# Rebalancing two on-chip rings and the transfer order in a matmul-scale-add kernel: a 16-tile x ring with casts six tiles ahead, a 32-tile add_value ring, eight-tile transfers

## The chip, the cores and the metric

One core of one Trainium2 chip. The time is the device time of one execution in microseconds (us); where several runs were made, their median is given with the lowest and highest. The profile's span (first to last instruction) is 1.7 to 2.1 us shorter than the time. Kernels that are compared ran on the same chip in the same rounds where that is said, and otherwise the spread is told.

## The reference

```python
# x: 16 x 512 x 1024, weight: 1024 x 768, add_value: 16 x 512 x 768, all fp32
def reference(x, weight, scale, add_value):
    return (scale * np.matmul(x, weight) + add_value).astype(np.float32)
```

Flattened, x has 8,192 rows: 64 tiles of 128. All of x (33.6 MB), weight (3.1), add_value (25.2) and the result (25.2) cross the DMA engines once, 87.03 MB in all.

## The kernel before

All transfers go through one issuing queue (SyncE), in the order of a list. Each entry is an operand, its first tile and the number of tiles: x loads, w weight chunks, a add_value loads, o outputs, l and r the two column parts of the last tile's output.

```python
STREAM = [
    ("x", 0, 1), ("x", 1, 1), ("x", 2, 1), ("w", 0, 1), ("w", 1, 1), ("w", 2, 1),
    ("w", 3, 1), ("w", 4, 1), ("w", 5, 1), ("x", 3, 1), ("w", 6, 1), ("w", 7, 1),
    ("a", 0, 3), ("a", 3, 1), ("x", 4, 4), ("x", 8, 4), ("a", 4, 4), ("x", 12, 4),
    ("a", 8, 8), ("x", 16, 8), ("a", 16, 8), ("x", 24, 8), ("o", 0, 8), ("x", 32, 8),
    ("a", 24, 4), ("a", 28, 4), ("o", 8, 8), ("x", 40, 4), ("a", 32, 8), ("o", 16, 8),
    # ... the same pattern on to tile 63
]
X_SLOTS = 24      # ring of x tiles, fp32
A_SLOTS = 24      # ring of add_value tiles; the result is written in place
```

A step is one tile. TensorE transposes the next tile in the middle of a step (through PSUM, ScalarE copies it out); for pairs of tiles (14 and 15, 19 and 20, ...) VectorE does the transposing instead. GpSimd casts x to bf16 ahead of either.

```python
def step():
    t = done["step"]
    for j in range(KJ):                                   # 8 contraction steps
        if j == KJ // 2:
            if t + 1 not in in_pair:
                transpose(t + 1)                          # TensorE, needs the cast of t + 1
            cast_to(min(t + 2, done["x"] - 1))            # GpSimd, frees a slot of the x ring
            if t + 7 in PAIRS:
                cast_pair(t + 7)
        product(t, j, BOTH)                               # 512 + 256 columns
    finish(t, BOTH[0], 0, N)                              # VectorE: scale, add, into the a ring
    # VectorE turns a quarter of a coming pair
```

An x load waits until the tiles in its slots are cast; an add_value load waits until the outputs in its slots have left.

## Time and profile before

| | before |
|---|---|
| time (3 runs) | 211.96 us (211.57 to 212.16) |
| TensorE busy | 196.4 us, 93% of the span |
| DMA engines busy | 98.1% of 16 engines |
| first steady transposes on TensorE | 26.33 us |
| last output: issued, time to landing | 206.53, 3.0 us |

The lines behind this table are in the prediction below. Two resources are near full, so the question for any change is which of them sets the end.

### The profile page before, as it was taken

What the parts mean: (1) busy time and instruction counts of PE and PEld (TensorE: products, weight loads), DVE (VectorE), ACT (ScalarE), POOL (GpSimd) and SP (SyncE); (2) the same over time, 40 slices, a digit from 0 to 9 for tenths busy, and PEclk for the clock granted to TensorE, in tenths of its full rate; (3) what the DMA queues carried; (4) which work ended last, traced back from release to release, by engine and by line L of the source; (5) the groups of instructions that cost most, each with busy time, mean ns of one, the idle gap of its engine ahead of it and who ended that gap; (6) DMA issues with size and microseconds to landing.
All of it is one profiled execution on the core that took longest, in us unless ns stands there. A gap on an engine that the chain in (4) does not pass through costs nothing.

```text
span 210.4 us, 3034 instructions
## 1 busy us (share of the span) xinstructions
PE 196.4 (93%) x1218; PEld 119.5 (57%) x1218; DVE 131.0 (62%) x223; ACT 49.3 (23%) x52; POOL 63.8 (30%) x69
## 2 busy tenths in 40 slices
PE   7887099999999999999999999999999999999991
PEld 2444056665656566666566565656665665666650
DVE  1447212329969869649999499786984993332232
ACT  3503013323302303112113023031121130233320
POOL 1310253441090080540350901705407340233000
PEclk9999759999999999999999999999999999999997
DMA  6999999999999999999999999999999999999995
GB/s 220 391 417 439 417 422 434 445 455 427 405 455 431 406 444 442 395 413 444 416 417 410 439 413 442 417 419 428 411 455 408 448 408 438 434 406 428 430 405 202
DMA packets 6781, 87.22 MB, mean 414 GB/s; under 512 B 752, under 2 KB 880, under 8 KB 2928
## 3 DMA queue, kind: packets, MB, share of 16 engines
q1 hardware_dynamic: 6768, 87.03, 98.1%
q8 instruction: 9, 0.15, 0.3%
q14 instruction: 4, 0.03, 0.0%
HBM read 61.87 MB, written 25.17 MB: 414 GB/s over the span
## 4 chain that ended last, share of the span: by engine, by line
PE 85%; DMA 10%; SPq 1%; POOL 0%; ACT 0%; issue 0%; DVE 0%; POOLq 0%; ACTq 0%
PE mm L168 76%; PE tp L146 9%; DMA xs<-in_x_dram 7%; DMA ao<-in_weight_dram 4%; SPq L100 1%; SPq L248 1%; POOL xb L136 0%; ACT xt L152 0%; DVE ao L176 0%; POOLq L136 0%; ACTq L152 0%
## 5 line engine op out<-in xcount | busy, mean ns | idle before, releaser
L168 PE MATMUL mm<-w_bf,xt 128*128 128x512 bf16 (+1 forms) x736 | 130.0, 330 | 1.9 <-DVE w_bf L104 1.4
L168 PEld LDWEIGHTS <-xt 128*128 128x128 bf16 x736 | 69.2, 99 | 52.2 <-ACT xt L152 10.8
L176 DVE SCALAR_TENSOR_TENSOR ao<-mm,ao 128x768 f32<-128x768 f32 (+2 forms) x62 | 58.4, 945 | 60.8 <-PE mm L168 43.8
L152 ACT COPY xt<-tp 128x1024 bf16<-128x1024 bf16 (+1 forms) x49 | 46.6, 961 | 150.7 <-PE tp L146 150.7
L120 DVE STREAM_TRANSPOSE vt<-vx 32x256 f32<-32x256 f32 x144 | 62.7, 435 | 2.7 <-POOL vx L109 0.5
L136 POOL CAST xb<-xs 128x1024 bf16<-128x1024 f32 x43 | 43.6, 1040 | 45.8 <-PE tp L146 26.4
L168 PE MATMUL mm<-w_bf,vt 128*128 128x512 bf16 (+1 forms) x288 | 49.7, 326 | 0.0
L109 POOL CAST vx<-xs 128x1024 bf16<-128x1024 f32 x18 | 18.2, 1040 | 78.7 <-DVE vt L120 45.0
L168 PEld LDWEIGHTS <-vt 128*128 128x128 bf16 x288 | 28.1, 98 | 17.6
L146 PE MATMUL tp<-identity,xb 128*128 128x128 f32 x184 | 28.9, 282 | 6.5 <-POOL xb L136 5.8
L146 PEld LDWEIGHTS tp<-identity,xb 128*128 128x128 f32 x184 | 22.2, 145 | 13.1 <-POOL xb L136 6.2
L104 DVE CAST w_bf<-ao 128x768 bf16<-128x768 f32 x8 | 4.5, 565 | 4.7 <-DMA ao<-in_weight_dram 4.7
L94 PE MATMUL warm<-zeros 128*128 128x512 bf16 x10 | 4.4, 629 | 1.2 <-DVE zeros L82 1.2
L132 DVE CAST xb<-xs 128x512 bf16<-128x512 f32 x3 | 1.3, 427 | 5.4 <-DMA xs<-in_x_dram 5.4
L134 POOL CAST xb<-xs 128x512 bf16<-128x512 f32 x2 | 1.7, 866 | 5.2 <-DMA xs<-in_x_dram 5.2
L94 PEld LDWEIGHTS <-zeros 128*128 128x128 bf16 x10 | 1.3, 140 | 3.4 <-issue 2.2
L235 DVE TENSOR_TENSOR ao<-ao 128x768 f32<-128x768 f32 x3 | 2.7, 952 | 0.0
L204 DVE TENSOR_SCALAR ao<-mm 128x768 f32<-128x768 f32 x2 | 1.8, 953 | 1.1 <-PE mm L168 1.1
L134 ACT ACT_TABLE_LOAD x1 | 1.3, 1283 | 0.7 <-PEq L279 0.7
L134 ACT CAST xb<-xs 128x512 bf16<-128x512 f32 x1 | 0.6, 618 | 2.5 <-DMA xs<-in_x_dram 2.5
L201 ACT ACTIVATE ao<-mm 128x768 f32<-128x768 f32 x1 | 0.8, 817 | 0.0
L82 DVE MEMSET zeros<- 128x256 uint32 x1 | 0.3, 272 | 0.9 <-PEq L279 0.9
(6 smaller groups left out, 0.9 us busy)
## 6 DMA issues: line engine op xcount, KB each, us to landing
out_dram<-ao SPq DMA_DIRECT2D x7, 3072.0 KB, 23.5
xs<-in_x_dram SPq DMA_DIRECT2D x9, 2048.0 KB, 23.8
ao<-in_add_value_dram SPq DMA_DIRECT2D x6, 3072.0 KB, 12.4
xs<-in_x_dram SPq DMA_DIRECT2D x3, 4096.0 KB, 42.3
ao<-in_add_value_dram SPq DMA_DIRECT2D x3, 1536.0 KB, 16.7
ao<-in_weight_dram SPq DMA_DIRECT2D x8, 384.0 KB, 7.8
xs<-in_x_dram SPq DMA_DIRECT2D x4, 512.0 KB, 5.1
out_dram<-ao SPq DMA_DIRECT2D x1, 1536.0 KB, 10.6
```

Source lines behind the costliest of these rows:

```text
L94: nc.tensor.matmul(warm[:, 0:CUT], zeros[:, 0:P], zeros, start=True, stop=True)
L100: nc.sync.dma_start(ao[:, s, :], w_v[:, j // 2, j % 2, :])
L104: nc.vector.tensor_copy(w_bf[:, j + i, :], ao[:, s + i, :])
L109: nc.gpsimd.tensor_copy(vx[:, i, :], xs[:, (t0 + i) % X_SLOTS, :])
L120: nc.vector.transpose(vt[b:b + 32, :, 32 * a:32 * a + 32], pairs[32 * a:32 * a + 32, :, b:b + 32])
L134: other(xb[:, K // 2:K], src[:, K // 2:K])
L136: nc.gpsimd.tensor_copy(xb, src)
L146: nc.tensor.transpose(tp[:, c, :], pairs[:, c * P:(c + 1) * P], identity)
L152: nc.scalar.copy(dst[:, c:c + q, :, :], src[:, c:c + q, :, :])
L168: nc.tensor.matmul(mm_tiles[t, cols[0]][:, n0:n1], lhs(t, j), w_bf[:, j, n0:n1], start=(j == 0), stop=(j == KJ - 1))
L176: nc.vector.scalar_tensor_tensor(a, mm_tiles[t, part][:, n0:n1], float(scale), a, op0=mybir.AluOpType.mult, op1=mybir.AluOpType.add)
L235: nc.vector.tensor_add(ao[:, t, :], ao[:, EARLY_AT + t, :], ao[:, t, :])
```

## The change

The intent: the same SBUF with the two rings rebalanced. Casting six tiles ahead into seven bf16 buffers frees x slots early, so 16 fp32 slots do; the freed space makes the add_value ring 32 tiles. The transfers are made uniform, eight tiles each, and the head of the list is merged.

```diff
 STREAM = [
-    ("x", 0, 1), ("x", 1, 1), ("x", 2, 1), ("w", 0, 1), ... , ("w", 5, 1), ("x", 3, 1), ("w", 6, 1), ("w", 7, 1),
-    ("a", 0, 3), ("a", 3, 1), ("x", 4, 4), ("x", 8, 4), ("a", 4, 4), ("x", 12, 4),
-    ...
+    ("x", 0, 3), ("w", 0, 2), ("w", 2, 2), ("w", 4, 2), ("x", 3, 1), ("w", 6, 2),
+    ("a", 0, 3), ("x", 4, 4), ("a", 3, 1), ("x", 8, 4), ("a", 4, 4), ("x", 12, 4),
+    ("a", 8, 8), ("x", 16, 8), ("a", 16, 8), ("x", 24, 8), ("a", 24, 8), ("o", 0, 8),
+    ("x", 32, 8), ("a", 32, 8), ("x", 40, 8), ("o", 8, 8), ("x", 48, 8), ("a", 40, 8),
+    ("o", 16, 8), ("o", 24, 8), ("a", 48, 8), ("x", 56, 8), ("a", 56, 8), ("o", 32, 8),
+    ("o", 40, 8), ("o", 48, 8), ("o", 56, 4), ("o", 60, 1), ("o", 61, 1), ("o", 62, 1),
+    ("l", 63, 1), ("r", 63, 1),
 ]
-X_SLOTS = 24
-A_SLOTS = 24
+X_SLOTS = 16
+A_SLOTS = 32
+AHEAD = 6
@@
-    xb_pool = ... bufs=3
+    xb_pool = ... bufs=7
@@
-                    cast_to(min(t + 2, done["x"] - 1))
+                    cast_to(min(t + AHEAD, done["x"] - 1))
```

## The prediction

> **What bounds the kernel now.** I read the page first: its engine shares, its 40-slice picture and its DMA queue table.
>
> ```profile
> PE 196.4 (93%) x1218; PEld 119.5 (57%) x1218; DVE 131.0 (62%) x223; ACT 49.3 (23%) x52; POOL 63.8 (30%) x69
> ...
> DMA  6999999999999999999999999999999999999995
> ...
> q1 hardware_dynamic: 6768, 87.03, 98.1%
> ```
>
> Two resources are full at once: TensorE for 93% of the span, the 16 DMA engines for 98.1% (206.4 of 210.4 us). The DMA row has no slice below 9 except the first and the last, so no gap in the transfers is there to be closed. TensorE has its gap at the front. The chain of waits, in order of time, shows it:
>
> ```profile
> 3.73 7.51 DMA ao<-in_weight_dram
> 11.26 13.83 DMA xs<-in_x_dram
> 25.24 1.05 POOL xb L136
> 26.33 1.11 PE tp L146 x4
> 27.45 4.31 PE mm L168 x16
> 31.76 0.44 PE tp L146 x4
> 32.19 2.63 PE mm L168 x16
> ```
>
> The first four-tile x transfer lands at 25.09 us (11.26 + 13.83). GpSimd casts tile 4, TensorE transposes it at 26.33, and from there TensorE runs almost without a break to 206.05; over 40 to 200 us the stretch table gives 159.83 us busy of 160. The first step is slow (4.31 instead of 2.63 us), at a clock of 0.50 between 25 and 30 us.
>
> Which of the two sets the end is read from the tail. The last output (128 KB) is issued at 206.53, after the last matmul and VectorE's last add. The DMA view of 206.4 us to the end says:
>
> ```profile
> DMA packets 363, 0.59 MB, mean 129 GB/s; under 512 B 47, under 2 KB 175, under 8 KB 363
> ...
> out_dram<-ao SPq DMA_DIRECT2D x1, 128.0 KB, 3.0
> ```
>
> Only 0.13 MB is issued in this stretch, but 0.59 MB still has to start: 0.46 MB stands ahead of the last transfer. At the 425 GB/s of the stretch 5 to 205 us that is 1.1 of its 3.0 us to landing. So with an empty queue the compute side alone would have landed near 206.53 + 3.0 - 1.1 = 208.4; the DMA queue makes it 209.5. **The DMA engines are the bound, by about 1.1 us over TensorE.** Both have to move for a gain above that.
>
> The longest waits in the issuing queue look alarming and are not:
>
> ```profile
> SPq L254 <- DMA out_dram<-ao: 118.6, 5, 32.3
> SPq L262 <- DVE ao L176: 34.2, 7, 9.0
> ```
>
> The first is an add_value load waiting until the output in its slots has left. Meanwhile earlier transfers are still being moved: x transfers take 24 to 42 us from issue to landing, of which a 2 MB one needs 5 us at 425 GB/s. Waiting in the issuing queue costs nothing while that backlog lasts.
>
> **What the Trainium skill says.** "DMA: Bandwidth & Descriptors", Specifications, gives a fabric ceiling of 435 GB/s. The trace agrees: 425 GB/s is held for 200 us, so at most 2% is to be won from the transfers by any means. "Perfetto Trace Analysis", What "DMA-bound" means, says that for a bound on the DMA engines large descriptors matter. The trace has the size of it, in the packet records: a 3,072-byte packet takes 121 ns in the median, 4,096 bytes 159, 12,288 bytes 460, 24,576 bytes 912, 32,768 bytes 1,214. That is a line: 8.4 ns a packet and 27.2 bytes per ns. "TensorE: Matmul & The Clock Gate", Part 1, says the clock drops after an idle window of about 3.4 us; here TensorE idles 5.8 us before 26.33 and the clock is 0.50 after it. "SBUF — State Buffer", Who interferes with whom, lets GpSimd and VectorE block each other on a shared port in some operations. I see nothing of that: GpSimd's cast is 1,040 to 1,042 ns in all 61 instances although VectorE is 62% busy. Moving casts earlier should not lengthen them.
>
> **The change part by part.**
>
> *Transfers.* Bytes stay the same. Before there are 47 transfers; after it 38: x goes from 16 to 11, weights from 8 to 4, add_value from 11 to 10, outputs from 12 to 13 (tiles 60 and 61 part). A transfer has 128 rows, so 8 packets on each of 16 engines, plus a semaphore packet of 9 ns. Nine fewer take 9 x (8 x 8.4 + 9) = 0.69 us off every engine's work. This lies directly on what sets the end: 209.5 becomes about 208.8.
>
> *Head.* The first x transfer is now 1.5 MB, so its casts start near 7 us (2.5 us later than tile 0's at 4.50). The weights come in pairs at nearly the same times as before, and the last still lands near 16 us, since the bytes ahead are the same. So the head's matmuls end near 19 us either way. The four add_value tiles used to be ahead of the first four-tile x; now the fourth goes behind it. That brings it forward by 0.375 MB, 0.97 us by the landings of like transfers, and and the head has six fewer transfers ahead of it, 0.46 us. TensorE's stream starts 1.4 us earlier, near 24.9. A shorter idle could also keep some clock: up to 1.7 us, the excess of 4.31 over 2.63. So compute alone would land at 207.0 or earlier (208.4 - 1.4), which is now 1.8 us inside the DMA bound. Most of it is not cashed in.
>
> *Casts six ahead.* The number of casts (43 + 18, 1,040 ns each) is the same; GpSimd is at 30%. Of the idle time of TensorE only 5.8 us is put down to a cast, and that is the one at 26.33, set by the landing. Worth 0 by itself; it makes a ring of 16 possible: a slot is free six tiles ahead of use, so 16 + 6 = 22 tiles of reach stand against 24 + 2 = 26.
>
> *Add_value ring of 32.* It breaks the wait of 118.6 us in part: tiles 24 to 31 no longer wait for the first output. Their load moves from 81 us to near 43. Worth 0 while the queue is never empty, but VectorE's waits for add_value (13.6 us in 4 cases, longest 4.2) shrink or move.
>
> **Does the queue ever run dry?** This decides between a small gain and a loss. I walked the new order by hand with first in, first out at the rates above and TensorE steps of 2.63 or 3.07 us. The tight places are where a load waits with little behind it. x 48 to 55 needs the casts of tiles 32 to 39, of which pair 39 and 40 waits for VectorE to turn pair 34, so it is issued near 114 us; the queue has work until about 120. Add_value 40 to 47 waits for output 8 to 15, landing near 122; x 48 fills the queue until about 130. x 56 and add_value 48 come near 146, work lasts until about 152. Each has 5 to 8 us in hand. The one data wait that can touch TensorE is add_value 40 to 47, landing near 139 when step 40 is done near 136; three PSUM buffers cover that by 2 to 3 us, but VectorE turns pair 44 behind it, which leaves under 1 us before step 44 needs it.
>
> **Rivals.**
> 1. *TensorE takes over or its head gain shows in full.* If the tail backlog were a small thing, the end would follow TensorE: 1.4 us, with the clock up to 3 us earlier, 209 to 210.5. The 0.46 MB ahead of the last output speak against it. The bytes cannot go faster.
> 2. *The smaller x ring starves the queue.* x loads in pieces of eight wait for eight casts. With 5 to 8 us in hand, a step or two of delay is absorbed; only a chain of delays at 114 or 146 us would open a gap, costing 2 to 5 us, 213 to 217.
> 3. *The late add_value 40 blocks VectorE and then TensorE.* The kernel before has the like: VectorE waited 4.24 us at 187 and TensorE did not stop. Costs 1 us of TensorE at most, hidden by the 1.8 us.
> 4. *Larger transfers in the tail or head cost latency.* The outputs of the tail are split finer, not coarser; the head has slack. Near zero.
>
> **Range and chances.** The span falls by 0.7 us, from 210.4 to 209.7; the measured time from 211.96 to **211.2 us** after rounding. The low end, 209.9, is rival 1 in part, with the slowest DMA engine faring better: in the tail the semaphore of the last of the 16 comes 1.3 us after the median one, which may differ by program. The high end, 212.3, is no gain and a scatter like the 211.57 to 212.16 of before. Faster by over 2% would need 207.7, beyond what 87 MB allow at the ceiling together with the head: 0.02. Slower by over 2% needs 216.2, a dry queue for 4 us: 0.05. Within 2%: 0.93.
>
> **What will show it.** Right: 9 x (128 + 16) = 1,296 fewer packets, DMA share near 98% with no slice below 9 inside; the first step's transposes near 24.9 us; TensorE ending near 204.6; the last output landing 3.5 us or more after its issue, behind a larger backlog. Wrong: a slice of the DMA row under 9 near 115 to 122 or 146 to 152 (rival 2), a TensorE gap near 139 to 146 (rival 3), or a last output that lands 2 us after issue, which would say that the transfers were not the bound. A longer median packet time for the 32,768-byte rows would break the packet sum.

## The result, and the profile after

The changed kernel takes 210.96 us (210.62 to 211.10, 4 runs), the kernel before in the same rounds 211.99 us (211.57 to 212.16). The ratio is 0.9952, 95% interval 0.9933 to 0.9971. Ratios here are the mean time of one kernel's runs over that of the other's of the same rounds, so not quite the ratio of the medians.

From the page of the changed kernel: TensorE's busy time, the DMA row of the 40 slices, and the queue's packets and share.

```profile
PE 196.4 (94%) x1218; PEld 119.5 (57%) x1218; DVE 131.1 (63%) x223; ACT 49.3 (24%) x52; POOL 63.2 (30%) x69
...
DMA  6999999999999999999999999999999999999993
...
q1 hardware_dynamic: 5472, 87.03, 97.7%
```

The work of TensorE is the same, and again no slice of the DMA row inside is below 9. The packets fell from 6,768 to 5,472, the 1,296 that nine fewer transfers make. The share fell by little, but of a shorter span: 97.7% of 209.2 us is 204.4 us, against 206.4 before.

The chain of waits of the changed kernel at the start of the steady stream:

```profile
20.67 2.61 DVE ao L235 x3
23.29 1.02 POOL xb L136
24.36 0.66 PE tp L146 x4
25.01 4.28 PE mm L168 x16
29.29 0.44 PE tp L146 x4
29.73 2.63 PE mm L168 x16
```

TensorE's stream starts at 24.36 us, 1.97 earlier. The line ahead of the cast names VectorE, but what the cast needs is the x transfer, which the trace has landing at 23.21. The first step is still slow (4.28 us), the next ones take 2.63 us as before. TensorE ends its matmuls at 203.6 instead of 206.0 us; VectorE's last add comes right behind, in the kernel before and then in the changed kernel:

```profile
206.07 0.42 DVE ao L176
...
203.61 0.42 DVE ao L176
```

The DMA view of the changed kernel from 203.9 us, just before its last output is issued at 204.06, to the end:

```profile
DMA packets 449, 0.81 MB, mean 132 GB/s; under 512 B 58, under 2 KB 186, under 8 KB 449
...
out_dram<-ao SPq DMA_DIRECT2D x1, 128.0 KB, 4.1
```

Now 0.81 MB still has to start when the last 0.13 MB is issued (0.59 MB before), and the last output takes 4.1 us (3.0 before). TensorE finished 2.4 us earlier; the last output landed only 1.34 us earlier (208.20 against 209.54). The rest of TensorE's gain went into a longer queue.

### The profile page after: what moved, and what is told of

Read it like the earlier page. It is cut to its first block, busy times and chain, and to the rows that moved or that the text cites. A ratio compares the mean times of both kernels' runs of the same rounds, so it can differ in the third digit from the quotient of the medians.

```text
span 209.2 us, 2988 instructions
## 1 busy us (share of the span) xinstructions
PE 196.4 (94%) x1218; PEld 119.5 (57%) x1218; DVE 131.1 (63%) x223; ACT 49.3 (24%) x52; POOL 63.2 (30%) x69
## 3 DMA queue, kind: packets, MB, share of 16 engines
q1 hardware_dynamic: 5472, 87.03, 97.7%
## 4 chain that ended last, share of the span: by engine, by line
PE 90%; DMA 3%; DVE 2%; ACT 1%; POOL 0%; issue 0%; ACTq 0%; POOLq 0%
PE mm L168 80%; PE tp L146 10%; DMA xs<-in_x_dram 3%; DVE ao L235 1%; ACT xt L152 1%; DVE ao L204 1%; POOL xb L136 0%; DVE xb L132 0%; DVE ao L176 0%; ACTq L152 0%; POOLq L136 0%
## 5 line engine op out<-in xcount | busy, mean ns | idle before, releaser
L152 ACT COPY xt<-tp 128x1024 bf16<-128x1024 bf16 (+1 forms) x49 | 46.6, 961 | 146.0 <-PE tp L146 146.0
L136 POOL CAST xb<-xs 128x1024 bf16<-128x1024 f32 x43 | 43.2, 1040 | 56.2 <-DMA xs<-in_x_dram 46.5
L109 POOL CAST vx<-xs 128x1024 bf16<-128x1024 f32 x18 | 18.3, 1040 | 53.8 <-DVE vt L120 44.7
L146 PE MATMUL tp<-identity,xb 128*128 128x128 f32 x184 | 28.3, 277 | 5.4 <-POOL xb L136 3.0
L146 PEld LDWEIGHTS tp<-identity,xb 128*128 128x128 f32 x184 | 21.7, 143 | 12.1 <-POOL xb L136 3.4
L132 DVE CAST xb<-xs 128x512 bf16<-128x512 f32 x3 | 1.9, 696 | 5.6 <-DMA xs<-in_x_dram 5.6
```

Of the source, the lines that this page charges most:

```text
L109: nc.gpsimd.tensor_copy(vx[:, i, :], xs[:, (t0 + i) % X_SLOTS, :])
L136: nc.gpsimd.tensor_copy(xb, src)
L146: nc.tensor.transpose(tp[:, c, :], pairs[:, c * P:(c + 1) * P], identity)
L152: nc.scalar.copy(dst[:, c:c + q, :, :], src[:, c:c + q, :, :])
```

## The experiments

Theory A: the DMA engines are the bound, and a transfer costs its bytes plus a small fixed cost for each packet. Theory B: TensorE's stream is the bound, and its earlier start is the gain. Two questions came up on the way: what the cast-ahead is worth (theory C), and what scatters the kernel before (D and E).

### Which resource sets the end: three cuts

Each run takes work from one side of the changed kernel, or from both. Their outputs are wrong, which doesn't matter for the times.

```diff
     def product(t, j, cols):
+        end = KJ - 2 if 20 <= t < 40 else KJ - 1      # e1, e3
+        if j > end:
+            return
...
         elif op == "a":
+            if s == 40:                               # e2, e3
+                continue
```

> The changed kernel with the last of the eight contraction steps left out for tiles 20 to 39 (results of these tiles wrong on purpose): 20 x 0.33 = 6.6 us less TensorE work, the same transfers. Theory A (the DMA engines are the bound): the time stays at 210.9 us within 0.4. Theory B (TensorE's stream is the bound): it falls by 2 us or more, up to 6.6.

> The changed kernel without the load of add_value tiles 40 to 47 (wrong on purpose): 3.1 MB, 7.3 us of all DMA engines, less; TensorE's work the same. Theory A: the time falls until TensorE takes over, by the share of the last output's 4.1 us to landing that is queue, about 2.0 to 2.4 us, to 208.6 to 209.0, and the last output lands about 2 us after its issue. Theory B: no change.

> Both cuts of the first two runs together (wrong on purpose). Theory A: now both bounds move, the time falls by 5 to 7 us, more than the sum of the two single cuts. Theory B: falls by as much as with TensorE's cut alone.

| run | TensorE's matmuls | transfers | time (4 runs) | against 210.93 |
|---|---|---|---|---|
| changed kernel, once more (6 runs, other rounds) | | | 210.93 (210.63 to 211.05) | |
| e1 | -6.6 us | | 210.89 (210.69 to 210.98) | 0.0 |
| e2 | | -3.1 MB | 208.46 (208.19 to 208.69) | -2.5 |
| e3 | -6.6 us | -3.1 MB | 205.91 (205.72 to 206.19) | -5.0 |

The DMA view of e2 from 203.4 us, just before its last output is issued at 203.55, to the end:

```profile
DMA packets 289, 0.39 MB, mean 60 GB/s; under 512 B 33, under 2 KB 161, under 8 KB 289
...
out_dram<-ao SPq DMA_DIRECT2D x1, 128.0 KB, 1.8
```

With TensorE's work cut the time does not move. With the transfers cut it falls, to a little under the 208.6 to 209.0 us expected, until the tail queue is gone: the last output lands 1.8 us after its issue, with its own and the previous tile part's bytes alone left to start. Both cuts together give twice the sum of the single ones. Theory A holds and B falls: the DMA engines are the bound, with 2.5 us to TensorE's bound behind it.

The cut of 6.6 us did not make TensorE's stream 6.6 us shorter. In e3 (as in e1) the steps that transpose the next tile still follow each other every 3.07 us, because TensorE now waits for ScalarE's copy of the transposed tile:

```profile
92.83 0.60 PE L146 MATMUL tp<-identity,xb 128*128 128x128 f32 x4
...
94.59 1.48 PE L171 MATMUL mm<-w_bf,xt 128*128 128x512 bf16 x8 [0.18 <-ACT xt L152]
95.90 0.60 PE L146 MATMUL tp<-identity,xb 128*128 128x128 f32 x4
```

Only the eight steps of this stretch in which TensorE transposes nothing get shorter: 8 x 0.33 = 2.6 us by estimate. That is what e3 shows (its last output is issued at 201.10 us, 2.45 us before that of e2), and why it gains 5.0 us and not up to 7. In e1 TensorE is 2.3 us ahead at step 38 and loses it again near 140 us, behind add_value 40 to 47. So B was tested with 2.3 us, of which nothing was left in the time.

### What a packet costs: the same bytes in more transfers

```diff
-    ("a", 8, 8), ("x", 16, 8), ...
+    ("a", 8, 4), ("a", 12, 4), ("x", 16, 4), ("x", 20, 4), ...      # all 20 eight-tile transfers
```

> The changed kernel with each of its 20 eight-tile transfers issued as two of four tiles: bytes and order the same, 20 more transfers. Packet theory (8.4 ns for each packet plus 9 ns for each transfer on every engine): 20 x 0.076 = 1.5 us longer, 212.4 us. Rival (only bytes count, and the gain of the change came from the earlier start of TensorE): no change within 0.3 us.

It took 212.12 us (211.99 to 212.31), 1.23 us over e1 of the same rounds and 1.2 over the changed kernel. The packet theory's 1.5 us is right in kind and a quarter too large. The packet records show the engines' mean busy time up by 1.6 us (206.26 against 204.62 in the changed kernel's second profile); why not all of that reaches the time is not shown. The rival, that only bytes count, falls.

### The parts of the change alone

e5 is the changed kernel again; e6 the kernel before with the new head of the list (its first two lines in the diff above); e7 the changed kernel with the old head; e8 the changed kernel with five further merges (and a line of the head's test that the merged x load needs).

```diff
 e8:
+    ("x", 0, 4), ("w", 0, 2), ("w", 2, 2), ("w", 4, 2), ("w", 6, 2),
+    ("x", 4, 4), ("a", 0, 4), ("x", 8, 4), ("a", 4, 4), ("x", 12, 4),
...
-    ("o", 56, 4), ("o", 60, 1), ("o", 61, 1), ("o", 62, 1), ("l", 63, 1), ("r", 63, 1),
+    ("o", 56, 6), ("o", 62, 1), ("o", 63, 1),
```

> The changed kernel once more, beside the parts of the change on the same chip: 1.0 us under the kernel before, 0.6 to 1.3.

> The kernel before with the changed head alone (first x tiles in one transfer, weights in pairs, the fourth add_value tile behind the first four-tile x): six transfers fewer, TensorE starts about 2 us earlier. Packet theory: 6 x 0.076 = 0.46 us under the kernel before. TensorE theory: 1.4 to 2 us under it.

> The changed kernel with the old head: three transfers fewer than before in the middle and the tail, TensorE starts as late as before. Packet theory: 3 x 0.076 = 0.23 us under the kernel before, and together with the head alone the whole of the change. TensorE theory: as the kernel before.

> The changed kernel with five more transfers merged (x 0 to 3 in one, add_value 0 to 3 in one, outputs 56 to 61 in one, tile 63 in one), the first four-tile x ahead of add_value. Packet theory: 5 x 0.076 = 0.38 us under the changed kernel, 210.5. Rival: the coarser tail leaves the queue empty and the end waits for TensorE; as the changed kernel or slower by up to 1 us.

| run, same chip and rounds | time (6 runs; before 11) | ratio to before, 95% interval |
|---|---|---|
| before | 212.35 (211.15 to 213.94) | |
| e5 changed kernel | 210.93 (210.63 to 211.05) | 0.9933 (0.9892 to 0.9974) |
| e6 new head alone | 212.90 (211.72 to 213.83) | 1.0023 (0.9978 to 1.0068) |
| e7 all but the head | 211.47 (211.26 to 211.76) | 0.9963 (0.9925 to 1.0001) |
| e8 five more merges | 210.99 (210.55 to 211.19) | 0.9937 (0.9899 to 0.9975) |

By medians the changed kernel gains 1.42 us on the kernel before in these rounds (0.6 to 1.3 expected), and e7 gains 0.88 us where its three transfers make 0.23. So the new middle may be worth more than its packets; e7's interval (a gain of 0 to 1.6 us) leaves it open.

Adding the head to e7 gives 0.54 us (e5), near the 0.46 us of six transfers. Adding it to the kernel before (e6) gives nothing measurable, but the interval (a gain of 0.5 to a loss of 1.4 us) doesn't exclude the 0.46 us either. The one trace of e6 has its last landing at 209.08 us, 0.46 earlier than the first profile of the kernel before, which would fit. A line of its waits has doubled (the kernel before, then e6):

```profile
DVE ao L176 <- DMA ao<-in_add_value_dram: 13.6, 4, 4.2
...
DVE ao L175 <- DMA ao<-in_add_value_dram: 27.1, 6, 6.7
```

VectorE waits 27.1 us for add_value (13.6 before): tiles 24 and up still wait in the 24-tile ring for the first output, and a TensorE that starts earlier only meets them earlier. VectorE turns pairs late behind that wait, and the trace shows TensorE stopping 0.8 us for a turned pair at 102.3 us. (Another stop, of 0.8 us at 57.6 us, is not the ring's: e9 has it too, with the 32-tile ring.) Whether the wider ring is what lets the head pay is not shown. In this trace TensorE keeps most of its lead: the last output is issued at 205.12 us, against 206.53 before.

The second finding is the scatter. Kernels with the old middle (before, e6) spread over 2.1 to 2.8 us; those with the new one (e5, e7, e8) over 0.4 to 0.6 us.

e8 is a version meant to beat both. Its profile seems to agree with the packet theory (span 208.8 against 209.2 and 209.3 us), but the profiled run is the fastest of its six; the runs do not agree, 210.99 against 210.93 us. Its trace also has what the rival expected: the engines stand without a packet for 1.1 us, mean of the 16, between 196 and 200 us, where the changed kernel has no such gap. Whether it is faster stays open; it is no worse.

### What the cast-ahead is worth

```diff
-AHEAD = 6
+AHEAD = 2
-    xb_pool = ... bufs=7
+    xb_pool = ... bufs=3
```

> The changed kernel with the casts only two tiles ahead and three cast buffers, as before, but the 16-tile x ring and the new order kept. The slots of x 40 to 47 and 48 to 55 come free later; worked out by hand their loads are issued 1.0 and 1.5 us before the queue runs empty, where the changed kernel has 14 and 6 us. Theory C (casting ahead is worth only the cover that it gives the queue): 0 to 1 us over the changed kernel, with more scatter. Rival (casting ahead feeds TensorE): 2 us or more. Rival (worth nothing): as the changed kernel, with its scatter of 0.5 us.

It took 214.58 us (214.38 to 216.09, 5 runs), ratio to before in the same rounds 1.0152 (1.0114 to 1.0190), and 3.65 us over the changed kernel, which ran in other rounds. The size is that of the first rival, far over theory C's 0 to 1 us; the mechanism is theory C's. The issuing queue of e9 and of the changed kernel, each from 100 us on, shows the mechanism (start, length, what is issued):

```profile
101.77 0.33 SPq L248 DMA_DIRECT2D xs<-in_x_dram  x1
102.15 0.42 SPq L262 DMA_DIRECT2D out_dram<-ao  x1
121.53 0.33 SPq L248 DMA_DIRECT2D xs<-in_x_dram  x1
```

```profile
88.71 0.67 SPq L248 DMA_DIRECT2D xs<-in_x_dram  x1
89.43 0.42 SPq L262 DMA_DIRECT2D out_dram<-ao  x1
114.53 0.33 SPq L248 DMA_DIRECT2D xs<-in_x_dram  x1
```

x 40 to 47 goes out at 101.77 instead of 88.71, when the transfer ahead of it lands at 104.80. That leaves 3.0 us of cover, and it lands at 117.46 instead of 114.43. The stretch tables of e9 and then the changed kernel (columns: stretch, length, busy us of TensorE, weight loads, VectorE, ScalarE, GpSimd, clock, DMA share, GB/s):

```profile
100.00:120.00 20.00, 20.00 (x130) 12.38 (x129) 14.00 (x26) 3.04 (x3) 7.24 (x8) 1.00 0.98 383
120.00:140.00 20.00, 19.83 (x128) 12.09 (x127) 14.73 (x27) 5.06 (x5) 6.48 (x7) 1.00 1.02 405
140.00:152.00 12.00, 7.71 (x49) 4.48 (x47) 7.63 (x13) 1.01 (x1) 2.46 (x3) 1.00 0.92 393
```

```profile
100.00:120.00 20.00, 20.00 (x130) 12.43 (x128) 15.66 (x28) 3.04 (x3) 9.51 (x10) 1.00 1.01 431
120.00:140.00 20.00, 19.83 (x127) 12.03 (x126) 14.10 (x26) 5.06 (x5) 5.03 (x5) 1.00 0.99 426
140.00:152.00 12.00, 12.00 (x78) 7.48 (x77) 11.34 (x21) 2.02 (x2) 4.98 (x5) 1.00 1.01 432
```

The rate falls from 431 to 383 GB/s while the DMA share stays at 0.98: the engines count as busy, but single packets take up to 1.3 us longer. TensorE loses nothing there that the changed kernel does not lose. From 140 us it loses 4.3 us, because add_value 40 to 47 is late (landing at 143.77 instead of 138.75) and VectorE holds up a PSUM buffer and pair 44 behind it. So casting ahead feeds TensorE next to nothing directly (it waits for a cast once, 0.3 us at 76.4 us); it keeps loads going out early enough.

### How much must stand in the queue

If that reading is right, less cover alone must cost time, with the casts left as they are. e10 and e12 put part of an x load behind the add_value load that waits for an output, in two places.

```diff
 e10:
-    ("x", 32, 8), ("a", 32, 8), ("x", 40, 8), ("o", 8, 8), ("x", 48, 8), ("a", 40, 8),
+    ("x", 32, 4), ("a", 32, 8), ("x", 36, 4), ("x", 40, 8), ("o", 8, 8), ("x", 48, 4), ("a", 40, 8), ("x", 52, 4),
 e12: the same with ("x", 32, 2) ... ("x", 34, 6) and ("x", 48, 2) ... ("x", 50, 6)
```

> The changed kernel with x 32 to 39 and x 48 to 55 each in two transfers, the second half behind the add_value load that waits for an output: at that wait only a 2 MB transfer is left in the queue, as in the kernel before, not 4 MB; add_value still comes early. Packet theory alone: 2 x 0.076 = 0.15 us over the changed kernel and its scatter of 0.5 us. Theory D (the thin cover at these waits is what makes the kernel before scatter up to 213.9 us): runs above 212 us come back here. Rival E (late add_value through the 24-tile ring makes it scatter): no such runs.

> The kernel before once more, for a second profile of it: if the profiled run is one of the long ones (above 212.3 us), theory D expects late packets or a gap of the DMA engines at 105 to 110, 125 to 130, 150 to 155 or 175 to 180 us, rival E expects gaps of TensorE behind VectorE's waits for add_value.

> As the thin variant, but with only two x tiles (1 MB, 2.4 us at 425 GB/s) left in the queue at the waits of add_value 32 and 40 for their outputs. TensorE's inputs all come as early as or earlier than in the changed kernel, so TensorE should not wait; two more transfers. Theory D (a wait in the issuing queue costs time as soon as less than some 3 to 5 us of transfers stand behind it, since a new transfer takes over 1 us from issue to first packet and the fastest engines are 1 to 2 us ahead of the slowest): 0.5 to 2 us over the changed kernel with late packets at 88 to 92 and 122 to 126 us. Rival (only the slowest engine counts, and it has work): packet theory alone, 2 x 0.076 = 0.15 us, 211.1, with the changed kernel's scatter of 0.5 us.

Cover is the time from the issue of such a waiting load to the landing of the transfer ahead of it, read from the traces; the smallest of a kernel is given.

| kernel | smallest cover | time (5 or 6 runs) |
|---|---|---|
| changed kernel (e5) | 7.2 us | 210.93 (210.63 to 211.05) |
| e10 | 4.8 us | 211.19 (210.82 to 212.25) |
| before, four places | 4.8 us | 212.07 (211.33 to 212.44) in e11, 211.49 (211.19 to 213.16) in the 11 runs beside it |
| e9 | 3.0 us | 214.58 (214.38 to 216.09) |
| e12 | 2.4 us | 215.77 (215.60 to 216.20) |

The stretch tables of e12 and of the changed kernel over the two places where e12 is thin:

```profile
86.00:91.00 5.00, 4.95 (x33) 3.18 (x33) 4.55 (x8) 0.00 (x0) 3.37 (x4) 1.00 0.94 347
...
120.00:130.00 10.00, 9.95 (x66) 6.21 (x65) 9.21 (x18) 3.04 (x3) 3.41 (x4) 1.00 0.86 337
```

```profile
86.00:91.00 5.00, 5.00 (x34) 3.08 (x33) 4.35 (x8) 0.00 (x0) 2.68 (x3) 1.00 1.01 431
...
120.00:130.00 10.00, 10.00 (x65) 6.04 (x64) 7.67 (x14) 3.04 (x3) 2.49 (x3) 1.00 1.00 428
```

e12 loses 4.8 us for moving three quarters of an x load behind another transfer, twice. Its expected late packets are there, at 89 and at 126 us. The expectation was 0.5 to 2 us; the loss is larger: packets are late again at the next changes of transfer, near 113 us (ten packets by 0.9 us or more) and 140 us, and TensorE then waits in turn, 4.5 us in four places. Why packets are late there, 20 us later and with work in the queue, I did not find.

The test is not of cover alone, because an operand does come late, against the expectation. x 34 to 39 land at 105.53 us (97.43 in the changed kernel), so the casts of pair 34 start at 105.68 instead of 99.52 us and VectorE waits 5.7 us for them. Two of TensorE's four waits, 2.4 us, are behind that pair. What does belong to the thin queue is in the packet records. At 89.0 us only 5 of the 16 engines have a packet, at 126.0 us one (all 16 at both times in the changed kernel). Cover counts to the landing on the last engine, and the first run dry sooner: from 88.0 us on, while the last lands at 90.52; the first packet of the load issued at 88.14 starts at 89.10. Between 3 and 200 us the engines stand without a packet for 2.0 us in e12, 1.0 in e9, 0.3 in the kernel before and 0.0 in the changed kernel, mean of the 16.

e10 gave one run above 212 us of six, as theory D asked, and 0.11 us in the median beyond its 0.15 us of packets. That speaks for D and is thin evidence. e11 was to show a long run of the kernel before; the profiled one took 212.29 us, just under the limit that I had set, and has the late packets where D has them, on the add_value load issued at 105.5 us (three of them 0.9 to 1.0 us late, near 108) and again near 114. It has no gap of TensorE that the first profile lacks, so E gets nothing from it. But its last landing is only 0.1 us later than in the first profile, whose run took 212.22 us and was as long: there is no profile of a short run to compare. **So a cover of 3.2 us and less is shown to leave engines idle and packets late; how much of the lost time is its own, in e12, is open, and so is what 4.8 us cost. That it also makes the kernel before scatter is not shown.**

## Why the prediction was right

- *The bound.* It said that the DMA engines lead TensorE by about 1.1 us. e1 to e3 show the kind of bound directly, for the changed kernel; there the lead is 2.5 us (predicted 1.8), near the 2.3 us of queue that the tail loses in e2. The prediction's estimate that 1.1 of 3.0 us were queue leaves 1.9 us for an empty one; e2 has 1.8.
- *Nine fewer transfers, 0.69 us.* The packet records give it exactly: summing 8.4 ns a packet and 27.17 bytes per ns (27.2 in the prediction) over all packets of each kernel gives 203.78 and 203.10 us for an engine. Measured in time it was 1.03 us. The remaining 0.3 us was not in the sum. What the records show besides is the excess of packets over that law: 2.6 us for an engine before, 1.3 after (2.7 in e11, 1.5 in e5). The prediction treated the old queue as never hampered because no slice fell below 9. That step was too coarse: a late packet counts as busy. The size of this term, and that all of the 0.3 us is it, stay unproven. That the number came so near is in part luck: the kernel before had medians of 211.40 to 212.35 us in the sets of rounds here, the changed kernel 210.93 and 210.96.
- *The head.* TensorE was to start near 24.9 us and did at 24.36; the x transfer landed 1.9 us earlier, not 1.4, partly because the 16 engines finished it within 0.3 us of each other (0.8 before). The clock did not profit: the first step took 4.28 us, at a clock of 0.66 between 25 and 30 us. It could have: in e2, with 3.02 us of idle before it instead of 3.04, the clock stayed at 1.00. As predicted, most of the lead was not cashed in.
- *The last output* was to land 3.5 us or more after its issue: 4.1 us.
- *Casts and rings, worth 0 by themselves but making the small ring possible.* Right, and e9 gives the other half: with the casts two tiles ahead the same order and rings lose 3.65 us. The casts did not get longer (1,040 to 1,042 ns in all 61); e3 and e9 have one each that did, of 1.72 and 1.76 us, while VectorE added tiles. Whether the wider add_value ring is worth 0 with the new head as well, e6 leaves open.
- *The queue never runs dry; 5 to 8 us in hand.* Right: between 3 and 200 us the engines stand without a packet for 0.0 us. The cover read from the trace is 7.2 us or more, issue by issue near the times given (x 48 at 114.5, add_value 40 at 121.8, add_value 48 at 146.0 us). Rival 2 put a dry queue at 213 to 217 us; e9 and e12, where engines do run dry, took 214.6 and 215.8.
- *Rival 3*, late add_value 40 to 47 reaching TensorE, did not happen: it landed at 138.75 (139 predicted) and TensorE has no gap there. In e9, 5 us later, it did.

## What to carry to other kernels

When two resources are near full, look at the last transfer: the part of its time to landing that is queue is the lead of the DMA engines over the compute side, and speeding up the compute side only lengthens that queue, or has it wait for a load (e1). In a kernel bound by DMA, count packets, and for every load that waits in the issuing queue count how many microseconds of transfers stand ahead of it. Here 7.2 us lost nothing, 3.2 us and less did, and 4.8 us is open. A feature "worth nothing" on the critical path, like casting further ahead here, can be what pays for that cover, so test it by taking it away from the finished kernel.

## What the Trainium skill lacked or had wrong

- "DMA: Bandwidth & Descriptors", Bandwidth, gives 78% of peak for 1 MB transfers and asks for 1 MiB or more. Its table is for transfers issued from GpSimd. In the full queue here, issued from SyncE, the 384 KB weight transfers' packets of 3,072 bytes took 121 ns, 406 GB/s over 16 engines; what they cost beyond their bytes is 0.076 us each, by the packet law, and 20 more transfers cost 1.2 us (e4).
- No page tells how much must be queued ahead of a waiting load. Here 7.2 us of cover was enough; with 3.0 and 2.4 us the kernel took 3.65 and 4.8 us longer (e9, e12; not all of it by the cover alone).
- "Perfetto Trace Analysis", DMA Engine Tracks, says that slices of a DMA engine show actual busy time without idle. Packets that ran up to 1.3 us over their usual length in e9, between 100 and 120 us, counted as busy: share 0.98 at 383 GB/s, against 1.01 at 431.
- "TensorE: Matmul & The Clock Gate", Part 1, puts the fall of the clock at an idle window of about 3.4 us. Here it fell after shorter idles too. In every run in which TensorE was idle for 3.04 us or more before its steady stream it fell (0.66 between 25 and 30 us in the changed kernel, after 3.04 us), in none with 3.02 us or less (1.00 in e2, after 3.02 us). An idle of 3.04 us cannot hold a whole window of 3.4 us; what did set it is open.
- No page tells how long a block of instructions that is fetched keeps a DMA engine, or what a data transfer loses by it. The page of the profile counts nine packets on queue 8, of the kind it calls instruction; in the trace each is 16 KB and takes 1.0 to 1.1 us, one every 20 us. After the first, at 28.0 us, one engine was 1.5 us behind the other fifteen (x 8 to 11 of the changed kernel: fifteen done by 29.08, the last at 30.57 us), and the landing is that of the last. That this packet made it late is inferred from the time.
